# The twelve score matmuls of a pair of heads as one entry of the scheduler

## The chip, the cores and the metric

The kernel runs on one core of a Trainium2 chip. The metric is the device time of one execution in microseconds; lower is better. The engines of the core that matter here are TensorE (PE in the profile; its weight loads are PEld), VectorE (DVE), ScalarE (ACT), GpSimd (POOL) and SyncE (SP), which issues most of the DMAs. Each works through its own list of instructions in order, and semaphores make an instruction wait for results of other engines.

## What is computed

Two layers of a transformer encoder on 256 tokens of width 1024. Each layer is a mixer with three groups of attention heads of width 64, followed by a gated feed-forward part with a small convolution.

```
for l in range(DEPTH):                      # 2 layers
    # mixer: 4 neighbourhood heads (a), 6 dilated-window heads (d), 6 grouped-query heads (c)
    h = rms_norm(x, n1);  proj = h @ w_in_l
    qa, ka, va, qd, kd, vd, qc, kc, vc = jnp.split(proj, cuts, axis=-1)
    # per head: q and k are normalised (d and c also rotated), then
    #   s = q k^T * scale (+ bias or mask);  p = softmax(s);  o = p v
    mix = jnp.concatenate([rms_norm(out_a, ...), rms_norm(out_d, ...), rms_norm(out_c, ...)], axis=-1)
    x = x + mix @ w_out_l
    # feed-forward
    h = rms_norm(x, n2);  g, u = jnp.split(h @ w_gu, 2, axis=-1)
    g = depthwise_conv_centred(g, cw, cb)
    x = x + (gelu(g) * u) @ w_dn
```

Everything is float32. The kernel reaches that accuracy with matmuls on the type float32r: each operand is split into a high part and a remainder (hi and lo), and a product is the sum of hi x hi, hi x lo and lo x hi.

## The kernel before

**A planner orders all the work.** The kernel's code doesn't call the engines. `Plan.add` (L232) records each operation as an entry: its engine, its assumed duration (`cost`, L348), the earlier entries that it depends on, and its rank, which is its place in the program, moved back where the code says `later(n)`. `Plan.order` (L277) then simulates the engines. Again and again it looks at all entries whose predecessors are placed, and takes the one that can start earliest; among those that can start at the same time, the one of lowest rank. `emit` (L340) issues the operations in that order. So the order on each engine is fixed when the program is built, from assumed durations.

**Slots.** Tiles come from pools with a fixed number of slots. The slots of a pool are given out in a fixed turn, that of the tiles' first use in the program: an entry that would be the first user of a tile is not placed before all earlier tiles of that pool have their slot and one is free (L299 to L307). PSUM has two pools of four slots: `psa` for the accumulators of projections, and `psw` (tag `w`) for everything short-lived: the scores of a head (`s_`), the transposed probabilities (`tp_`), the output of a pair of heads (`o_`), transposes of q and k, and the gate and up products of the feed-forward part.

**A layer's mixer.** The projections are computed in the order dq, dk, dv, cq, ckv, aqk, av. A generator (`filler`, class `Weave`) yields them, and after them the output projections of the first two head groups (d and c), so that these matmuls stand between the steps of the attention. Attention goes through 16 heads, in the order d (6), c (6), a (4), by the loop at L1091. At step i (even) `scores(i)` writes the scores of heads i and i+1, `heads[i-1].turn()` transposes the probabilities of the head before, and `weigh(i-2)` multiplies those of the head before that with the values; each pair of heads shares an output tile, which `mixed` takes out. After the last head come `group_rstd(2)`, the output projections of the third group, and the feed-forward part.

**The scores of a pair** (L1023 to L1038). Two heads lie beside each other on the 128 partitions of q and k: the first on partitions 0 to 63 (`LOW`), the second on 64 to 127 (`HIGH`). Each head has 2 blocks of 128 queries, and each block three products, so 6 matmuls with 64 rows of contraction and 256 columns; the program lists the twelve of a pair with the two heads alternating. To the planner they are twelve separate entries with an assumed 60 ns each (the two lines in `cost` that test for rows up to `HD`). The first matmul of each head is the first user of that head's `psw` tile. `softens` then does the softmax: on DVE bias, sum and maximum (or only the maximum, for group c), on ACT the exponentials and the division by the sum.

Of the kernel before, what the change touches and what calls it, by code (L numbers as in the profile page):

```python
# [18 lines left out]
P = 128  # L19
S = 256  # L20
NT = S // P
D = 1024
KD = D // P
HD = 64
# [52 lines left out]
class View:  # L77


    def __init__(self, tile_, dtype, rows, idx, steps):  # L80
        self.tile, self.dtype, self.rows, self.idx, self.steps = tile_, dtype, rows, idx, steps
        self.shape, self.covers = (rows[1] - rows[0],) + idx.shape, None
# [111 lines left out]


class Op:
    __slots__ = ("engine", "method", "args", "kw", "ns", "size", "tiles", "first", "before", "after", "left", "at", "rank")


class PlanEngine:  # L200
# [14 lines left out]

class Plan:
    def __init__(self, tc):
        self.tc, self.ops, self.shift = tc, [], 0
        for name, short in (("tensor", "PE"), ("scalar", "ACT"), ("vector", "DVE"), ("gpsimd", "POOL"), ("sync", "SP")):
            setattr(self, name, PlanEngine(self, short, getattr(tc.nc, name)))  # L220

# [4 lines left out]
    def later(self, n):  # L226
# [2 lines left out]
        yield  # L229
        self.shift -= n  # L230

    def add(self, engine, method, args, kw):  # L232
        o = Op()
        o.engine, o.method, o.args, o.kw = engine, method, args, kw
        i = len(self.ops)
        o.rank = i + self.shift
        views = [v for v in (*args, *kw.values()) if isinstance(v, View)]
        outs = [v for v in args[:1] if isinstance(v, View)]
        if method == "tensor_tensor_reduce":
            outs.append(args[-1])  # L240
        if "accum_out" in kw:
            outs.append(kw["accum_out"])
        ins = [v for v in views if not any(v is w for w in outs)]
        if method == "matmul" and not kw["start"]:
            ins.append(args[0])
        o.ns, o.size = cost(engine.name, method, args, kw, ins)
        o.before, o.after, o.first, o.tiles = set(), [], [], []
        for v in ins + outs:
            t = v.tile
            if t not in o.tiles:  # L250
                o.tiles.append(t)
                t.users += 1
                if t.users == 1:
                    o.first.append(t)
        meets = lambda a, b: a[0] < b[1] and b[0] < a[1] and any(s < f and r < e for s, e in a[2] for r, f in b[2])
        holds = lambda a, b: a[0] <= b[0] and b[1] <= a[1] and len(a[2]) == 1 and a[2][0][0] <= b[2][0][0] and b[2][-1][1] <= a[2][0][1]
        for v in ins:
            f = v.footprint()
            met = {j for j, g in v.tile.writes if meets(f, g)}
            assert met, "read before written"  # L260
            o.before |= met
        for v in outs:
            f, t = v.footprint(), v.tile
            o.before |= {j for j, g in t.writes + t.reads if meets(f, g)}
            t.writes = [(j, g) for j, g in t.writes if not holds(f, g)]
            t.reads = [(j, g) for j, g in t.reads if not holds(f, g)]
        for v in ins:
            v.tile.reads.append((i, v.footprint()))
        for v in outs:
            v.tile.writes.append((i, v.footprint()))  # L270
        o.before.discard(i)
        o.left = len(o.before)
        for j in o.before:
            self.ops[j].after.append(i)
        self.ops.append(o)

    def order(self):  # L277
        ops = self.ops
        turns = {}
        for o in ops:  # L280
            for t in o.first:
                t.turn = turns.get(t.pool, 0)
                turns[t.pool] = t.turn + 1
                t.left = t.users
        free = dict.fromkeys(("PE", "ACT", "DVE", "POOL", "SP"), 550.0)
        ring = wires = 0.0
        ready = {e: [] for e in free}
        for i, o in enumerate(ops):
            o.at = 0.0
            if not o.left:  # L290
                ready[o.engine.name].append(i)
        done = []
        while len(done) < len(ops):
            best = None
            for e, r in ready.items():
                for i in r:
                    o = ops[i]
                    at = max(o.at, free[e])
                    for t in o.tiles:  # L299
                        s = t.pool  # L300
                        if t.slot is not None:
                            at = max(at, t.since)
                            continue
                        if t.turn != s.given or not s.free:
                            at = None
                            break
                        at = max(at, min(s.free)[0])  # L307
                    if at is not None and (best is None or (at, o.rank) < best[:2]):
                        best = (at, o.rank, i)
            at, _, i = best  # L310
            o = ops[i]
            e = o.engine.name
            ready[e].remove(i)
            done.append(i)
            for t in o.tiles:
                if t.slot is None:
                    s = t.pool
                    s.given += 1
                    place = min(s.free)
                    s.free.remove(place)  # L320
                    t.since, t.slot = place
            free[e] = end = at + o.ns
            if o.method == "dma_start":
                ring = max(at + 60, ring) + 460
                wires = max(ring + 550, wires) + o.size / 360
                end = wires + 900
            for t in o.tiles:
                t.left -= 1
                t.until = max(t.until, end)
                if not t.left:  # L330
                    t.pool.free.append((t.until + 170, t.slot))
            for j in o.after:
                a = ops[j]
                a.at = max(a.at, end + (170 if o.method == "dma_start" else HANDOVER.get((e, a.engine.name), 0)))
                a.left -= 1
                if not a.left:
                    ready[a.engine.name].append(j)
        return done

    def emit(self):  # L340
        real = lambda v: v.bind() if isinstance(v, View) else v
        with self.tc.manual_schedule():
            for i in self.order():
                o = self.ops[i]
                getattr(o.engine.real, o.method)(*map(real, o.args), **{k: real(v) for k, v in o.kw.items()})  # L345


def cost(engine, method, args, kw, ins):  # L348
# [6 lines left out]
    n = out.width()  # L355
    psum = any(v.tile.pool.psum for v in ins)
    if engine == "PE":
        if method == "transpose":
            return 110, 0
        n = args[2].width()  # L360
        if args[1].dtype == F32:
            return 108, 0
        if args[1].rows[1] - args[1].rows[0] <= HD:
            return 60, 0
        return (0.4444 * n + 4.6 if args[1].dtype == F32R else 210), 0
    if engine == "ACT":
        extra = 93 * sum(isinstance(kw.get(k), View) for k in ("scale", "bias")) + 90 * ("accum_out" in kw)
# [1 line left out]
    if engine == "DVE":  # L369
        if method in ("reduce_sum", "reduce_max"):  # L370
            n = args[1].width()
# [14 lines left out]
def encoder_kernel(  # L386
# [21 lines left out]
    nc = Plan(tc)  # L408
# [39 lines left out]
    with nc.later(1000):  # L448
        for _ in range(WARM):
            nc.tensor.matmul(  # L450
                wps.rearrange("p (a b) -> p a b", b=P), warm, warm.unsqueeze(1).to_broadcast([P, WARM_W // P, P]),
                start=True, stop=True,
# [15 lines left out]
    LOW, HIGH = slice(0, HD), slice(HD, P)  # L468
# [203 lines left out]
    for l in range(DEPTH):  # L672
# [350 lines left out]
        def scores(i):  # L1023

            two = heads[i : i + 2]
            group = two[0].group
            qs, ks = turned[group + "q"], turned[group + "k"]
            sps = [psw.tile([P, NT, S], F32, tag="w", name=f"s_{h.name}") for h in two]
            for t in range(NT):
                c = slice(t * P, (t + 1) * P)  # L1030
                for n, (x, y) in enumerate(((0, 0), (0, 1), (1, 0))):
                    for h, rows_, sp in zip(two, (LOW, HIGH), sps):
                        nc.tensor.matmul(
                            sp[:, t], qs[x][rows_, h.h // 2, c], ks[y][rows_, h.kv if group == "c" else h.h // 2],
                            start=n == 0, stop=n == 2,
                        )
            for h, sp in zip(two, sps):
                h.softens(sp)  # L1038

# [82 lines left out]
        _, r2 = mean_squares(f"n2{l}")  # L1122
# [188 lines left out]
```

## Time and profile before

| | |
|---|---|
| median of 3 runs | 633.17 us (632.21 to 633.89) |
| the profiled execution | 633.06 us, span 631.3 us, mean clock 0.997 |
| PE busy | 620.5 us (98% of the span), 3496 matmuls |
| DVE busy | 484.9 us (77%), 984 instructions |
| ACT busy | 429.6 us (68%), 1064 instructions |
| POOL busy | 72.2 us (11%) |
| score matmuls, both layers | 192 (120 of groups d and a, 72 of group c), 25.9 us busy |

In rows of the timeline the first number is the start in us from the beginning of the span, the second the length, then the engine, the line, the operation, the tile written, the tiles read, the shape, and how many instructions the row merges. All operations are issued at L345, so the line tells nothing here, and the tile names do: `psw_w` is a slot of the short-lived PSUM pool, `act_ko,act_qo` are keys and queries of groups d and a, `act_kc,act_qc` those of group c; a score matmul is recognised by its shape 64*128. `psa_a<-wp_hi,act_hT` is a projection, `psa_a<-wp_hi,act_mixT_hi` an output projection, `psw_w<-const_ident,act_s2k` a transpose of probabilities, and `psw_w<-act_ch,const_v` a weigh matmul. Matmuls overlap in the pipeline, so the distance from start to start says what one costs, not its own length.

### The profile page before, as it was taken

Reading aid. Unit: us, or ns where it says so; the run is one execution under the profiler, and the core shown is the slowest. Engines: PE = TensorE matmul, PEld = TensorE weight load, DVE = VectorE, ACT = ScalarE, POOL = GpSimd, SP = SyncE. Lnnn points to the kernel's source line nnn. Section 1 sums busy time; section 2 is a strip of 40 time slices with the busy share of each in tenths; the row PEclk is TensorE's granted clock in tenths of the full one; section 3 lists DMA queues with packets and bytes.
Section 4 is the critical chain, followed back from the end, with each engine's and each line's share of the span. In section 5 each row is a group of like instructions: output and inputs, shape, how many; then the busy total and the mean of one; then the engine's idle time right before and its main releaser. Section 6 shows DMA issues by size and latency. Waiting matters only on the chain.

```text
span 631.3 us, 9829 instructions
## 1 busy us (share of the span) xinstructions
PE 620.5 (98%) x3496; PEld 534.7 (85%) x3496; DVE 484.9 (77%) x984; ACT 429.6 (68%) x1064; POOL 72.2 (11%) x123
## 2 busy tenths in 40 slices
PE   8989999999999999999999999999999999999997
PEld 6988888878888888888899988888888888888886
DVE  4677987988777777777877798867887777777775
ACT  7578988767655566565678899985866555665552
POOL 3823231120000000000014212111100000000000
PEclk9989999999999999999999999999999999999999
DMA  9879220956656555665444731208565555565511
GB/s 293 271 199 201 72 73 14 227 199 202 200 200 200 180 176 182 197 200 184 129 125 165 250 102 50 67 5 267 191 209 201 182 174 182 195 198 177 174 53 66
DMA packets 84837, 104.66 MB, mean 166 GB/s; under 512 B 13012, under 2 KB 72500, under 8 KB 84788
## 3 DMA queue, kind: packets, MB, share of 16 engines
q1 hardware_dynamic: 84244, 103.51, 52.0%
q8 instruction: 27, 0.44, 0.3%
q10 hardware_dynamic: 544, 0.52, 0.3%
q14 instruction: 22, 0.18, 0.1%
HBM read 102.98 MB, written 1.49 MB: 165 GB/s over the span
## 4 chain that ended last, share of the span: by engine, by line
PE 84%; DVE 7%; ACT 3%; POOL 3%; issue 1%; DMA 1%; SPq 0%; DVEq 0%; ACTq 0%
PE psw_w L345 46%; PE psa_a L345 38%; DVE wp_lo L345 3%; ACT act_s2k L345 1%; DVE const_x L345 1%; DVE act_s2k L345 1%; POOL small_rstd L345 1%; DMA const_x<-in_x_dram 1%; DVE act_hT L345 1%; ACT wp_hi L345 1%; ACT L345 1%; POOL small_ms L345 1%; DVE act_nab L345 0%; SPq L345 0%; DVE act_qo L345 0%
## 5 line engine op out<-in xcount | busy, mean ns | idle before, releaser
L345 DVE TENSOR_TENSOR wp_lo<-wp_raw,wp_hi 128x512 fp32r<-128x512 f32 (+2 forms) x348 | 245.0, 733 | 62.3 <-ACT wp_hi L345 60.2
L345 PE MATMUL psw_w<-act_hT,wp_hi 128*128 128x512 f32 x704 | 249.2, 398 | 0.6 <-DVE act_hT L345 0.6
L345 ACT CAST wp_hi<-wp_raw 128x512 fp32r<-128x512 f32 (+2 forms) x348 | 212.9, 661 | 30.6 <-PE psw_w L345 15.9
L345 PE MATMUL psw_w<-act_hT,wp_lo 128*128 128x256 f32 x704 | 196.7, 281 | 0.1
L345 PEld LDWEIGHTS psw_w<-act_hT,wp_hi 128*128 128x128 f32 x704 | 131.8, 188 | 32.7 <-DVE act_hT L345 1.0
L345 PEld LDWEIGHTS psw_w<-act_hT,wp_lo 128*128 128x128 f32 x704 | 132.9, 189 | 1.9 <-DVE wp_lo L345 0.6
L345 PE MATMUL psa_a<-wp_hi,act_hT 128*128 128x384 f32 (+2 forms) x448 | 115.8, 338 | 1.4 <-ACT wp_hi L345 1.4
L345 ACT COPY act_s2k<-psw_w 128x256 f32<-128x256 f32 x88 | 32.4, 373 | 78.2 <-PE psw_w L345 78.2
L345 PEld LDWEIGHTS psa_a<-wp_hi,act_hT 128*128 128x128 f32 x448 | 79.1, 191 | 5.3 <-ACT wp_hi L345 1.8
L345 PE MATMUL psa_a<-wp_lo,act_hT 128*128 128x384 f32 (+2 forms) x224 | 75.7, 338 | 1.1 <-DVE wp_lo L345 1.0
L345 PE MATMUL psa_a<-wp_hi,act_cl 128*128 128x512 f32 x176 | 68.7, 392 | 0.6 <-DVE act_cl L345 0.6
L345 PE MATMUL psa_a<-wp_hi,act_ch 128*128 128x512 f32 x176 | 69.1, 393 | 0.0
L345 PE MATMUL psa_a<-wp_lo,act_ch 128*128 128x512 f32 x176 | 68.6, 390 | 0.0
L345 DVE TENSOR_TENSOR act_s2k<-psw_w,act_s2k 128x256 f32<-128x256 f32 x88 | 36.6, 422 | 31.0 <-ACT act_s2k L345 30.2
L345 PEld LDWEIGHTS psa_a<-wp_lo,act_hT 128*128 128x128 f32 x224 | 42.8, 191 | 3.4 <-DVE wp_lo L345 2.1
L345 PEld LDWEIGHTS psa_a<-wp_hi,act_cl 128*128 128x128 f32 x176 | 33.0, 188 | 8.8 <-DVE act_cl L345 1.4
L345 PEld LDWEIGHTS psa_a<-wp_hi,act_ch 128*128 128x128 f32 x176 | 33.0, 188 | 7.1
L345 PEld LDWEIGHTS psa_a<-wp_lo,act_ch 128*128 128x128 f32 x176 | 33.1, 188 | 6.4
L345 DVE SCALAR_TENSOR_TENSOR act_s2k<-act_s2k,act_cw,act_s2k 128x255 f32<-128x255 f32 x88 | 36.8, 480 | 1.4 <-ACT act_s2k L345 1.3
L345 ACT ACTIVATE act_s2k<-act_s2k,act_cw 128x256 f32<-128x256 f32 x44 | 24.1, 596 | 12.3 <-DVE act_s2k L345 12.3
L345 POOL TENSOR_TENSOR small_rstd<-small_ms,const_mh 128x6 f32<-128x6 f32 (+2 forms) x26 | 31.8, 1224 | 2.2
L345 ACT ACTIVATE act_s2k<-act_s2k,small_rs 128x256 f32<-128x256 f32 x64 | 29.0, 507 | 2.7 <-DVE small_rs L345 2.5
(109 smaller groups left out, 765.1 us busy)
## 6 DMA issues: line engine op xcount, KB each, us to landing
wp_raw<-in_w_gate_up_dram SPq DMA_DIRECT2D x44, 1024.0 KB, 5.1
wp_raw<-in_w_down_dram SPq DMA_DIRECT2D x22, 1024.0 KB, 5.0
wp_raw<-in_w_in_dram SPq DMA_DIRECT2D x14, 768.0 KB, 5.7
wp_raw<-in_w_in_dram SPq DMA_DIRECT2D x8, 1024.0 KB, 7.8
wp_raw<-in_w_out_dram SPq DMA_DIRECT2D x8, 768.0 KB, 5.5
wp_raw<-in_w_out_dram SPq DMA_DIRECT2D x4, 512.0 KB, 3.9
act_nab<-dram_scr SPq DMA_DIRECT2D x4, 448.0 KB
out_dram<-const_x SPq DMA_DIRECT2D x4, 256.0 KB, 2.0
```

The source lines that it names most:

```text
L345: getattr(o.engine.real, o.method)(*map(real, o.args), **{k: real(v) for k, v in o.kw.items()})
```

## The change

An entry of the planner can now hold several calls. The context manager `together(ns)` collects the operations recorded inside it and enters them as one entry with a given duration; `emit` issues its calls one behind the other. The rest of `add` becomes `enter`. In `order`, an entry may be the first user of several tiles: it is placed only when it is the turn of all of them and as many slots are free, at the time at which the last of these is free. `scores` wraps the twelve matmuls of a pair in `together(910)`, and the 60 ns of `cost` go away, since nothing uses them any more.

```diff
+    @contextmanager
+    def together(self, ns):
+        self.burst = calls = []
+        yield
+        self.burst = None
+        engine, method, args, kw = calls[0]
+        outs, ins = [], []
+        for _, _, a, _ in calls:
+            if not any(a[0] is v for v in outs):
+                outs.append(a[0])
+            ins += a[1:]
+        self.enter(engine, method, args, kw, ins, outs, calls, ns)
+
     def add(self, engine, method, args, kw):
-        o = Op()
-        o.engine, o.method, o.args, o.kw = engine, method, args, kw
-        i = len(self.ops)
-        o.rank = i + self.shift
+        if self.burst is not None:
+            self.burst.append((engine, method, args, kw))
+            return
...
+    def enter(self, engine, method, args, kw, ins, outs, calls, ns):
+        o = Op()
+        o.engine, o.method, o.calls = engine, method, calls
+        i = len(self.ops)
+        o.rank = i + self.shift
+        o.ns, o.size = (ns, 0) if ns else cost(engine.name, method, args, kw, ins)
...
                     at = max(o.at, free[e])
+                    news = {}
                     for t in o.tiles:
                         s = t.pool
                         if t.slot is not None:
                             at = max(at, t.since)
                             continue
-                        if t.turn != s.given or not s.free:
+                        n = news.get(s, 0)
+                        news[s] = n + 1
+                        if t.turn != s.given + n or len(s.free) <= n:
                             at = None
                             break
-                        at = max(at, min(s.free)[0])
+                        at = max(at, sorted(s.free)[n][0])
...
-                getattr(o.engine.real, o.method)(*map(real, o.args), **{k: real(v) for k, v in o.kw.items()})
+                for engine, method, args, kw in self.ops[i].calls:
+                    getattr(engine.real, method)(*map(real, args), **{k: real(v) for k, v in kw.items()})
...
-        if args[1].rows[1] - args[1].rows[0] <= HD:
-            return 60, 0
...
-            for t in range(NT):
-                c = slice(t * P, (t + 1) * P)
-                for n, (x, y) in enumerate(((0, 0), (0, 1), (1, 0))):
-                    for h, rows_, sp in zip(two, (LOW, HIGH), sps):
-                        nc.tensor.matmul(
-                            sp[:, t], qs[x][rows_, h.h // 2, c], ks[y][rows_, h.kv if group == "c" else h.h // 2],
-                            start=n == 0, stop=n == 2,
-                        )
+            with nc.together(910):
+                for t in range(NT):
+                    c = slice(t * P, (t + 1) * P)
+                    for n, (x, y) in enumerate(((0, 0), (0, 1), (1, 0))):
+                        for h, rows_, sp in zip(two, (LOW, HIGH), sps):
+                            nc.tensor.matmul(
+                                sp[:, t], qs[x][rows_, h.h // 2, c], ks[y][rows_, h.kv if group == "c" else h.h // 2],
+                                start=n == 0, stop=n == 2,
+                            )
```

More of the change, by code (lines that the diff above doesn't have):

```diff
@@ L196 @@
 class Op:
-    __slots__ = ("engine", "method", "args", "kw", "ns", "size", "tiles", "first", "before", "after", "left", "at", "rank")
+    __slots__ = ("engine", "method", "calls", "ns", "size", "tiles", "first", "before", "after", "left", "at", "rank")
 class PlanEngine:
@@ L217, in __init__ @@
     def __init__(self, tc):
-        self.tc, self.ops, self.shift = tc, [], 0
+        self.tc, self.ops, self.shift, self.burst = tc, [], 0, None
         for name, short in (("tensor", "PE"), ("scalar", "ACT"), ("vector", "DVE"), ("gpsimd", "POOL"), ("sync", "SP")):
@@ L245, in add @@
             ins.append(args[0])
-        o.ns, o.size = cost(engine.name, method, args, kw, ins)
+        self.enter(engine, method, args, kw, ins, outs, [(engine, method, args, kw)], 0)
+    def enter(self, engine, method, args, kw, ins, outs, calls, ns):
[4 more added lines that the diff above has]
+        o.ns, o.size = (ns, 0) if ns else cost(engine.name, method, args, kw, ins)
         o.before, o.after, o.first, o.tiles = set(), [], [], []
@@ L343, in emit @@
             for i in self.order():
-                o = self.ops[i]
-                getattr(o.engine.real, o.method)(*map(real, o.args), **{k: real(v) for k, v in o.kw.items()})
+                for engine, method, args, kw in self.ops[i].calls:
+                    getattr(engine.real, method)(*map(real, args), **{k: real(v) for k, v in kw.items()})
 def cost(engine, method, args, kw, ins):
```

## The prediction

> **What bounds the kernel now.** I read the page's totals first, then the busy time of every engine over the two attention stages, then TensorE's (PE's) instructions in order of time, looking for the score matmuls.
>
> ```profile
> span 631.3 us, 9829 instructions
> PE 620.5 (98%) x3496; PEld 534.7 (85%) x3496; DVE 484.9 (77%) x984; ACT 429.6 (68%) x1064; POOL 72.2 (11%) x123
> ```
>
> ```profile
> 49.70:120.30 70.60, 70.60 (x477) 60.83 (x477) 59.70 (x164) 60.94 (x179) 18.09 (x30) 1.00 0.44 101
> 357.80:426.80 69.00, 68.73 (x474) 59.14 (x474) 57.29 (x162) 62.06 (x180) 13.33 (x19) 1.00 0.19 61
> ```
>
> The second pair of rows runs from the first score matmul of a layer to the last weigh matmul: length, then busy time of PE, weight loads, DVE, ACT, POOL, then clock and DMA. PE has no gap in layer 0 and 0.27 us in layer 1, at full clock (1.00). DVE is busy 85% and 83%, ACT 86% and 90%. So PE sets the pace, but ACT stands close behind.
>
> Now the score matmuls. They are the only ones on 64 rows; a pair of heads uses rows 0-63 and 64-127. Rows of the timeline give start, length, shape, count:
>
> ```profile
> 49.77 0.98 PE L345 MATMUL psw_w<-act_ko,act_qo 64*128 64x256 f32 x12
> 50.67 0.39 PE L345 MATMUL psa_a<-wp_hi,act_hT 128*128 128x256 f32 x1
> ...
> 59.33 0.97 PE L345 MATMUL psw_w<-act_ko,act_qo 64*128 64x256 f32 x6
> 60.24 0.33 PE L345 MATMUL psw_w<-const_ident,act_z 128*128 128x128 f32 x1
> 60.49 0.97 PE L345 MATMUL psw_w<-act_ko,act_qo 64*128 64x256 f32 x6
> ...
> 80.95 0.38 PE L345 MATMUL psw_w<-act_kc,act_qc 64*128 64x256 f32 x1
> ```
>
> Twelve matmuls that alternate between the two row halves last as long (0.98) as six of one head alone (0.97). One alone lasts 0.38, so a run costs about 0.26 fixed plus 0.12 for each step, and in an alternating run a step carries two matmuls. A pair broken into two runs of six therefore pays for twelve steps where six would do.
>
> **The change, part by part.** It makes the twelve one entry, which nothing can split, placed when both PSUM slots are free. No instruction is added or removed and no DMA is issued anew; the order of everything after the first changed pair is chosen anew.
>
> *Score matmuls on PE.* The same view, restricted to the tiles of the keys (first the d and a heads, then the c heads; length and PE busy time are the first two values after the stretch):
>
> ```profile
> 45.00:110.00 65.00, 7.09 (x60) 5.44 (x60) 0.75 (x2) 0.65 (x2) 1.00 0.41 98
> 345.00:420.00 75.00, 8.31 (x60) 6.27 (x60) 1.85 (x4) 1.63 (x4) 1.00 0.30 100
> ...
> 45.00:110.00 65.00, 6.49 (x36) 4.67 (x36) 0.73 (x2) 0.61 (x2) 1.00 0.41 98
> 345.00:420.00 75.00, 4.02 (x36) 3.01 (x36) 0.85 (x2) 0.73 (x2) 1.00 0.30 100
> ```
>
> Layer 0 spends 7.09 + 6.49 = 13.58 us on scores, layer 1 8.31 + 4.02 = 12.33. Eight whole runs at 0.98 are 7.84 a layer: 5.74 and 4.49 less. Read in order, the runs count 12 | 6, 6 | 12 | 7, 5 | 1, 2, 3, 1, 5 | 6, 6 | 12 | 4, 2, 6 in layer 0 (17 runs for 8 pairs) and 12 | 12 | 3, 3, 6 | 1, 11 | 1, 11 | 12 | 6, 6 | 5, 1, 6 in layer 1 (15).
>
> Each run also slows its neighbours:
>
> ```profile
> 84.61 0.28 PE L345 MATMUL psw_w<-act_cl,const_v 128*128 128x256 f32 x1
> 84.73 0.28 PE L345 MATMUL psw_w<-act_ch,const_v 128*128 128x256 f32 x1
> 84.93 0.85 PE L345 MATMUL psw_w<-act_kc,act_qc 64*128 64x256 f32 x5
> 85.72 0.39 PE L345 MATMUL psa_a<-wp_lo,act_hT 128*128 128x256 f32 x1
> 85.94 0.40 PE L345 MATMUL psa_a<-wp_hi,act_hT 128*128 128x256 f32 x2
> ```
>
> A 128x256 matmul normally gives way after 0.12 (84.61 to 84.73). Ahead of the run it takes 0.20, behind it 0.22, which is 0.08 + 0.10 more; the run's last 0.06 overlaps its successor (84.93 + 0.85 - 85.72). Net 0.12 a run. Nine runs fewer in layer 0 are 1.1, seven in layer 1 are 0.8. PE work falls by 5.74 + 1.1 = 6.8 and 4.49 + 0.8 = 5.3, together 12.1 us. This part I hold for nearly certain; it would be the gain if PE stayed without gaps.
>
> *Where PE would run dry.* The planner has filler matmuls (projections, output projections of the first two head groups). If the attention chain ends no earlier, the saving can only be spent on filler that is still left when the last weigh matmul is done:
>
> ```profile
> 120.22 0.28 PE L345 MATMUL psw_w<-act_ch,const_v 128*128 128x256 f32 x1
> 120.33 0.40 PE L345 MATMUL psa_a<-wp_hi,act_mixT_lo 128*128 128x512 f32 x1
> ...
> 125.80 0.39 PE L345 MATMUL psa_a<-wp_hi,act_mixT_lo 128*128 128x512 f32 x1
> ```
>
> ```profile
> 121.36 0.48 DVE L345 SCALAR_TENSOR_TENSOR act_mixT_lo<-psw_w,const_gains,act_mixT_hi 128x256 fp32r<-128x256 f32 x1
> ```
>
> ```profile
> 120.30:133.70 13.40, 11.97 (x49) 8.86 (x49) 3.54 (x5) 0.00 (x0) 1.00 0.84 288
> 426.75:440.00 13.25, 12.23 (x50) 9.04 (x50) 4.18 (x6) 0.00 (x0) 1.00 0.96 316
> ```
>
> The last fence counts the output-projection matmuls (first value in brackets) after the last weigh: 49 and 50. The third head group owns 24 of them (2 blocks x 2 token tiles x 2 halves x 3 products); 25 and 26 are filler. At 24 steps in 5.47 us (120.33 to 125.80), or 0.228 each, that is 5.7 and 5.9 us of work in hand. Without it PE would stand from 120.33 until the third group's operand is written, 121.36 + 0.48 = 121.84: 1.5 us. With a chain that ends when it ends now, the cover is 5.7 - 1.5 = 4.2 of 6.8 us and, with the same 1.5, 5.9 - 1.5 = 4.4 of 5.3 us: 8.6 us together.
>
> *The chain itself can move either way.* It may come earlier, since DVE now stands waiting for scores:
>
> ```profile
> DVE small_nm L345 <- PE psw_w L345: 3.2, 5, 1.5
> DVE act_s2k L345 <- PE psw_w L345: 2.8, 4, 1.9
> ...
> DVE act_s2k L345 <- PE psw_w L345: 4.0, 5, 1.3
> DVE small_nm L345 <- PE psw_w L345: 1.1, 3, 0.6
> ```
>
> (two rows of layer 0, two of layer 1: total, times, longest.) Those 6.0 and 5.1 us are enough to let the whole 12.1 through. It may come later, since the first head of a pair now waits for the second head's slot. Queued behind that wait are, in the fixed turn of the PSUM slots, the transposes of the head before and the next output tile; but they wait today too, until the second head has its slot. Only the first head's softmax is new among the late ones. While PE holds an entry no other work can cut in, at most 0.91 us (49.77 to 50.67). I take the two shifts as cancelling; the bounds are +3.5 us of gain (12.1 - 8.6) and the delays of the second rival.
>
> *Crowding.* ACT's 62.06 us in layer 1 would have to fit into 69.0 - 4.4 = 64.6 us (96%); layer 0's 60.94 into 66.4 (92%). What PE loses beside a full ACT one stretch shows:
>
> ```profile
> 358.00:368.00 10.00, 9.73 (x78) 8.80 (x78) 8.36 (x29) 9.97 (x34) 2.64 (x3) 1.00 0.21 65
> ```
>
> 0.27 us of PE lost in 10 us with ACT at 9.97. Over the seven such stretches of a layer it is at most 1.9. I take half, 0.9, for layer 1, and nothing for layer 0, whose ACT would be less full; bounds 0 and 3.8 for both.
>
> *Sum.* 8.6 - 0.9 = 7.7 us. The profiled execution took 633.06 us (631.3 of span and 1.8 around it), 0.11 under the median of the runs shown, 633.17. 633.06 - 7.7 = 625.4 us.
>
> **The rivals.** *First, the freed PE time is partly given back.* The last pair of a layer decides when the chain ends, and its first head starts later:
>
> ```profile
> 105.93 0.74 PE L345 MATMUL psw_w<-act_ko,act_qo 64*128 64x256 f32 x4
> 108.75 0.97 PE L345 MATMUL psw_w<-act_ko,act_qo 64*128 64x256 f32 x6
> ```
>
> ```profile
> 412.57 0.85 PE L345 MATMUL psw_w<-act_ko,act_qo 64*128 64x256 f32 x5
> 415.37 0.97 PE L345 MATMUL psw_w<-act_ko,act_qo 64*128 64x256 f32 x6
> ```
>
> The start of its second head lies 2.8 us after that of its first in both layers. If both chains end that much later, the cover shrinks to 1.4 + 1.6 = 3.0 us: 630.1 us. For it: DVE and ACT then get two softmaxes at once. Against it: the second head, which ends the chain, gets its slot no later than now. The Trainium skill speaks for this rival (TensorEngine Tiling (Array Packing), section Performance Considerations, PSUM Bottleneck): tiling speeds up TensorE but not the emptying of PSUM, which may become the bound; by that rule the gain goes only as far as ACT and DVE have room, and no run here shows it yet.
>
> *Second, slower: the delays add up.* PSUM slots are given in a fixed turn, so a late first head can delay its transposes and, through them, the next pair. In layer 0 the second head starts 1.2 us after the first in the second pair (59.33 to 60.49), 2.9 in the fifth and 2.8 in the eighth; in layer 1 it is 3.9 in the third, 2.8 in the eighth:
>
> ```profile
> 83.85 0.38 PE L345 MATMUL psw_w<-act_kc,act_qc 64*128 64x256 f32 x1
> ...
> 372.34 0.61 PE L345 MATMUL psw_w<-act_ko,act_qo 64*128 64x256 f32 x3
> 376.20 0.97 PE L345 MATMUL psw_w<-act_ko,act_qo 64*128 64x256 f32 x6
> ...
> 406.37 0.97 PE L345 MATMUL psw_w<-act_ko,act_qo 64*128 64x256 f32 x6
> 409.11 0.97 PE L345 MATMUL psw_w<-act_ko,act_qo 64*128 64x256 f32 x6
> ```
>
> With 2.7 us for layer 1's seventh pair that is 6.9 + 9.4 = 16.3 us. It turns the result once more than the 7.7 us of cover, 47% of it, reaches the ends of the chains; if 80% does, 13.0 - 7.7 = 5.3 us are lost: 638.4 us. Against it: pairs that stood whole today (49.77) had both slots free anyway, and DVE's waits for scores are spread out, none over 1.9 us.
>
> *Third, no change.* The runs become whole, but the new order delays other work (transposes and weigh matmuls behind an entry: 16 entries at up to 0.91 us, 14.6 us at the most) by as much as it saves: about 633 us. Against it: PE is never idle at these places, so what waits is replaced by filler.
>
> **How the numbers follow.** The forecast 625.4 us has 0.66; its own range goes from the full 12.1 us (621.0) to half the gain (629.2). The first rival has 0.15, the second 0.11, the third 0.08. A measurement of this kernel can't tell less than 0.3% (1.9 us) from no change. Faster by more: 0.66 + 0.15 = 0.81; within: 0.08; slower: 0.11. The range reaches from 620.5 (the full saving and layer 1's idle 0.27 with it) to 632.5, past the first rival and into the third; the second stays outside.
>
> **What would show it.** Timeline: sixteen rows of twelve 64x256 matmuls of 0.98 us, none shorter in count; score busy time 15.7 us instead of 25.9. PE busy over the whole page near 609, DVE and ACT unchanged in count. After the last weigh matmul, fewer than 25 filler matmuls remain; if none remain and PE waits there for the mixed output, the first rival holds. The forecast is wrong if PE shows gaps within the attention stage ended by ACT or DVE, or if the last weigh matmul of a layer lies further behind its first score matmul than the present 70.6 and 69.0 us.

## The result and the profile after

The changed kernel takes 622.2 us (median of 4 runs, 621.25 to 623.27) beside 633.04 us for the kernel before: a ratio of 0.983, interval 0.981 to 0.985, so 10.8 us less. 7.7 us were forecast. The profiled execution took 621.25 us, its span 619.5.

The page's totals after the change:

```profile
span 619.5 us, 9832 instructions
PE 607.6 (98%) x3496; PEld 525.3 (85%) x3496; DVE 482.5 (78%) x984; ACT 428.3 (69%) x1064; POOL 73.6 (12%) x123
```

The same number of instructions on each of these engines, and PE busy 12.9 us less, in a span that is 11.8 us shorter. Where it went shows when each layer's mixer is cut at the same two instructions in both kernels, the first score matmul and the first matmul of the feed-forward part. First the kernel before, then the changed one (stretch, length, then busy time and number of instructions of PE, weight loads, DVE, ACT, POOL):

```profile
49.77:133.66 83.89, 83.37 (x539) 71.28 (x539) 70.81 (x182) 67.42 (x195) 20.80 (x33) 1.00 0.50 131
357.88:439.93 82.05, 81.65 (x536) 69.72 (x536) 67.16 (x180) 68.60 (x196) 15.75 (x22) 1.00 0.31 102
```

```profile
47.63:125.90 78.27, 77.33 (x539) 66.30 (x538) 70.28 (x183) 67.81 (x196) 21.08 (x33) 1.00 0.60 144
350.86:428.14 77.29, 76.73 (x536) 66.47 (x536) 66.23 (x180) 67.70 (x196) 16.11 (x22) 1.00 0.34 108
```

PE executes the same 539 and 536 matmuls, 6.04 and 4.92 us faster. The stretches get shorter by 5.62 and 4.76 us, 10.4 together; PE's idle time in them rises only from 0.92 to 1.50 us. The score matmuls of the changed kernel, in the views in which the prediction read them (the d and a heads, then the c heads):

```profile
45.00:110.00 65.00, 4.89 (x60) 3.87 (x60) 0.84 (x2) 0.86 (x2) 1.00 0.51 120
340.00:410.00 70.00, 4.90 (x60) 3.87 (x60) 1.77 (x4) 1.70 (x4) 1.00 0.33 107
...
45.00:110.00 65.00, 2.93 (x36) 2.31 (x36) 0.84 (x2) 0.72 (x2) 1.00 0.51 120
340.00:410.00 70.00, 2.94 (x36) 2.33 (x36) 0.84 (x2) 0.75 (x2) 1.00 0.33 107
```

15.66 us in place of 25.9. Each pair is one row of twelve, for instance the first, the third last and the last pair of layer 0:

```profile
47.64 0.98 PE L368 MATMUL psw_w<-act_ko,act_qo 64*128 64x256 f32 x12
...
94.29 0.98 PE L368 MATMUL psw_w<-act_kc,act_qc 64*128 64x256 f32 x12
...
106.28 0.98 PE L368 MATMUL psw_w<-act_ko,act_qo 64*128 64x256 f32 x12
```

What else differs between the two profiles is a small loss and a difference that isn't the change's. The loss: from the first matmul of layer 0's feed-forward part to the first scores of layer 1 it takes 0.74 us longer (224.96 us, before 224.22). 0.54 us of this come before the second half of the normalised input is there: PE now waits for it behind five weight splits on DVE. Two views of the changed kernel, DVE and PE (in brackets the idle time ahead of the row and who ended it), then the same matmul in the kernel before:

```profile
127.61 3.09 DVE L368 TENSOR_TENSOR wp_lo<-wp_raw,wp_hi 128x512 fp32r<-128x512 f32 x5
130.61 1.65 DVE L368 SCALAR_TENSOR_TENSOR act_hT<-psw_w,const_gains,act_hT 128x256 fp32r<-128x256 f32 x4
```

```profile
131.15 0.50 PE L368 MATMUL psw_w<-act_hT,wp_hi 128*128 128x512 f32 x1 [1.29 <-DVE act_hT L368]
```

```profile
138.37 0.50 PE L345 MATMUL psw_w<-act_hT,wp_hi 128*128 128x512 f32 x1 [0.28 <-DVE act_hT L345]
```

The other difference: the first score matmul starts 2.13 us earlier (49.77, now 47.64). In one repeat of the changed kernel it starts at 48.30, and in two kernels with the same order of work up to that point at 49.80 and 51.03, so this start scatters by itself. The granted clock is part of it. Before and after, the stretch ahead of the first scores (the clock is the value behind POOL's bracket):

```profile
36.00:47.60 11.60, 11.60 (x62) 11.57 (x61) 9.81 (x21) 8.02 (x19) 1.44 (x3) 0.85 0.84 214
```

```profile
36.00:47.60 11.60, 11.60 (x70) 11.35 (x68) 9.54 (x21) 9.12 (x29) 1.87 (x5) 1.00 0.90 216
```

The kernel before was profiled with the clock at 0.85 there, the changed one at 1.00; if PE's work goes with the clock, that is (1.00 - 0.85) x 11.6 = 1.7 us, an estimate. The stages account for 10.38 - 0.74 = 9.64 us, which lies inside the interval (9.5 to 12.2 us). Below, a kernel is judged by its median and by the sum of its two stretches, which differs by 0.05 us between the two profiles of the changed kernel: 165.94 us before, 155.56 after, 155.61 in the repeat. Part of the scatter of the medians goes with the clock. With a mean granted clock below 0.998 the kernel before, as it ran beside the experiments, has a median of 633.6 us (32 executions), with a higher one 632.6 (9); the changed kernel and its repeat together have 623.6 (3) and 621.9 (5). At like clock that is 10.0 and 10.7 us less, from few executions.

### The profile page after: what moved, and what is told of

Its sections match the earlier page's. It is cut to its first block, busy times and chain, and to the rows that moved or that the text cites. A ratio compares the mean times of both kernels' runs of the same rounds, so it can differ in the third digit from the quotient of the medians.

```text
span 619.5 us, 9832 instructions
## 1 busy us (share of the span) xinstructions
PE 607.6 (98%) x3496; PEld 525.3 (85%) x3496; DVE 482.5 (78%) x984; ACT 428.3 (69%) x1064; POOL 73.6 (12%) x123
## 4 chain that ended last, share of the span: by engine, by line
PE 84%; DVE 7%; ACT 3%; POOL 3%; issue 2%; DMA 1%; SPq 0%; DVEq 0%; ACTq 0%
PE psw_w L368 45%; PE psa_a L368 39%; DVE wp_lo L368 3%; ACT act_s2k L368 2%; POOL small_rstd L368 1%; DVE const_x L368 1%; DVE act_s2k L368 1%; DMA act_s2k<-in_norm_g_dram 1%; DVE act_hT L368 1%; ACT L368 1%; POOL small_ms L368 0%; DVE act_z L368 0%; DVE act_qo L368 0%; POOL act_sck L368 0%; DVE act_cl L368 0%
## 5 line engine op out<-in xcount | busy, mean ns | idle before, releaser
L368 ACT ACTIVATE act_s2k<-act_s2k,act_cw 128x256 f32<-128x256 f32 x44 | 24.1, 596 | 12.9 <-DVE act_s2k L368 12.9
L368 ACT ACTIVATE act_s2k<-act_s2k 128x512 f32<-128x512 f32 x22 | 13.9, 632 | 22.3 <-DVE act_s2k L368 22.3
```

Of the source, the lines that this page charges most:

```text
L368: getattr(engine.real, method)(*map(real, args), **{k: real(v) for k, v in kw.items()})
```

## The experiments

Beside the repeat, only the first two variants below keep the changed kernel's order of everything else. Each of the others has an order of its own, and an order by itself moves the time by several us, as the experiments with the declared duration show. So a difference of 2 us between two orders doesn't prove its cause. What holds across all of them is PE's work: in the two stretches PE is busy from 153.7 to 166.3 us, and idle for 0.8 to 2.7 us in all kernels but one (4.3 us, declared with 720 ns).

**The same order of work without the alternation.** If the gain is PE time, it must go when the two heads no longer alternate, though everything else stays in its place.

```diff
             with nc.together(910):
-                for t in range(NT):
-                    for n, (x, y) in enumerate(((0, 0), (0, 1), (1, 0))):
-                        for h, rows_, sp in zip(two, (LOW, HIGH), sps):
+                for h, rows_, sp in zip(two, (LOW, HIGH), sps):
+                    for t in range(NT):
+                        for n, (x, y) in enumerate(((0, 0), (0, 1), (1, 0))):
```

> One entry per pair and both slots at once, as in the changed kernel, but within the entry all six matmuls of the first head come before the six of the second, so the two row halves no longer alternate. The declared 910 ns stays, so the order on every engine is that of the changed kernel. Theory (the gain is PE time, because alternating matmuls share a step): a run has 12 steps, 0.26 + 12 x 0.12 = 1.70 us in place of 0.98, 16 x 0.72 = 11.5 us more PE work than the changed kernel: 622.2 + 11.5 = 633.7, about the time of the kernel before. Rival (the gain comes from the order that the planner now finds, not from the alternation): 622 to 625.

Measured: 628.7 us, ratio 0.993 (0.990 to 0.995), stretches 159.95. By the medians more than half of the gain is gone, by the stretches 4.4 of 10.4 us, by the order of twelve matmuls alone. But it is some 6 us and not 11.5. The run is shorter than I had worked out:

```profile
51.03 1.32 PE L368 MATMUL psw_w<-act_ko,act_qo 64*128 64x256 f32 x12
```

1.32 us, not 1.70. With that the sum comes out between the two measures: 16 x 0.34 = 5.4 us, against 4.4 us in the stretches and 5.9 to 6.5 in the medians (622.8 and 622.2 for the changed kernel). The forecast time failed for its price of a run; the theory that PE time sets the pace stands, and the rival (622 to 625) is out.

**Where the short run comes from.** In the serial run three of the twelve starts coincide with another. Either PE itself takes matmuls of the other half ahead, or three overlap wherever the halves change.

```diff
             with nc.together(910):
                 for t in range(NT):
-                    for n, (x, y) in enumerate(((0, 0), (0, 1), (1, 0))):
-                        for h, rows_, sp in zip(two, (LOW, HIGH), sps):
+                    for h, rows_, sp in zip(two, (LOW, HIGH), sps):
+                        for n, (x, y) in enumerate(((0, 0), (0, 1), (1, 0))):
```

> The changed kernel with its twelve in blocks of three: three of the first head, three of the second, and again; the order of everything else is that of the changed kernel. The serial order of six and six took 1.32 us a run and not the 1.70 that twelve steps would give: three of its twelve starts coincide with another. Theory A (TensorE itself takes matmuls of the other half ahead, up to three behind a change of halves from the first to the second): nearly all find a partner, a run of 0.98 to 1.1 us, 622 to 624.5. Theory B (three coincide per run, wherever the halves change): 1.3 us a run and 628 to 629, like the serial order. Theory C (only neighbours in the list can coincide): three changes of halves, three coincidences, the same 1.3 us and 628 to 629; the starts in the trace tell B and C apart.

Measured: 623.5 us, ratio 0.984 (0.983 to 0.986), stretches 155.75. Theory A:

```profile
49.80 0.98 PE L368 MATMUL psw_w<-act_ko,act_qo 64*128 64x256 f32 x12
```

The starts of the twelve, read from the trace (us, from the first):

```
alternating     0.000 0.004  0.225 0.227  0.341 0.345  0.466 0.470  0.580 0.583  0.699 0.702
threes          0.000 0.010  0.223 0.233  0.340 0.350  0.465 0.475  0.579 0.589  0.698 0.708
six and six     0.000  0.223  0.340 0.348  0.465  0.571 0.579  0.690 0.698  0.808  0.928  1.048
```

Three and three pair off as completely as one and one. With six and six, the second half begins to pair at the third step. The record of a matmul doesn't name its half, so which two coincide is read from the lists. The lengths in the records agree with it: in each run just two are 0.38 us long, as the first of a half is, and these are the first two records of the alternating runs and the threes, but the first and the fourth (0.000 and 0.348) of six and six.

**The same serial entry, declared longer.** Does the planner's knowledge of the duration matter? Here the serial entry is declared longer (its real length turned out to be 1.32 us, so 1630 is too much).

```diff
-            with nc.together(910):
+            with nc.together(1630):
```

> The same as the serial entry, but declared with 1630 ns, about what it really takes, so the planner lays the rest around it accordingly. Theory: the PE work is that of the serial entry, so 632 to 634, at most 1.5 us better than with the wrong declaration. Rival (what matters is that the declared duration is right): clearly faster than the entry declared with 910 ns, 626 or less.

Measured: 631.1 us, ratio 0.996 (0.995 to 0.998), stretches 163.51: 2.4 us worse than the same run declared with 910. Its score matmuls take the same 21.2 us. But PE is busy for 160.81 us of the stretches against 159.12 with 910, and idle for 2.70 us against 0.83. So the rest of the order costs here: 1.7 us more busy time in other matmuls and 1.9 us more waits. The forecast range (632 to 634) was missed by 0.9 us; the rival (626 or less) is out.

**The kernel before with truer durations.** The 60 ns per matmul were too low for a run of one head (0.12 us a step); without the two lines a score matmul counts 118 ns.

```diff
-        if args[1].rows[1] - args[1].rows[0] <= HD:
-            return 60, 0
```

> The kernel before with one thing changed: the 60 ns that the planner assumes for a score matmul become 118, which is what one of a single head takes. Entries stay single. In this order the score matmuls stand in 30 runs (before 32) with 132 steps (before 146), 16 x 0.12 + ... of them: 30 x 0.38 + 132 x 0.12 = 27.2 us of PE against 29.7 before. Theory: 633.0 - 2.5 x 0.9 = 630.8 us. Rival (truer durations are the gain): 622 to 625. A rival that durations do nothing and the order only shifts: 633.

Measured: 632.7 us beside 633.6, ratio 0.999 (0.997 to 1.001), stretches 165.43. No difference that can be told, which is the last of the three expectations; the score matmuls take 24.5 us instead of 25.9. The theory's 630.8 was 2 us too low, and the rival that truer durations are the gain is out by 8 us.

**No joint wait: one entry per head.** This takes away what both of the prediction's rivals rest on, the first head's wait for the second head's slot.

```diff
-            with nc.together(910):
-                for t in range(NT):
-                    for n, (x, y) in enumerate(((0, 0), (0, 1), (1, 0))):
-                        for h, rows_, sp in zip(two, (LOW, HIGH), sps):
+            for h, rows_, sp in zip(two, (LOW, HIGH), sps):
+                with nc.together(910):
+                    for t in range(NT):
+                        for n, (x, y) in enumerate(((0, 0), (0, 1), (1, 0))):
```

> Each head is an entry of its own: its six matmuls stand together, and it takes only its own slot, so the first head never waits for the second head's slot; the halves don't alternate. In this order there are 23 runs and 192 steps: 23 x 0.38 + 192 x 0.12 = 31.8 us of PE, 14.2 more than the changed kernel, 2.7 more than the serial entry with both slots at once. If waiting for both slots costs nothing: 2.4 to 2.7 us above the serial entry declared truly, so 635 to 637. If the joint wait costs several us (the rivals of the prediction): at or below that entry's time, 633 or less.

Measured: 634.9 us, ratio 1.003 (1.002 to 1.004), stretches 167.74: slower than the kernel before, though no work can cut into a head's six. Its score matmuls take 26.4 us in 23 runs, those of the serial entry 21.2 us in 16; with 0.12 us a run the difference is 6.0 us of PE work. Beside the serial entry declared with 1630, 3.8 us are measured by the medians and 4.2 by the stretches, so by that comparison the joint wait costs some 2 us over 16 pairs. Beside the one declared with 910 it is 6.2 us, and the wait costs nothing. Two orders can differ by that much, so a cost of the joint wait isn't shown; a large one is out, and what it brings (the halves side by side) is worth more, even when the list is serial.

**Both slots at once, but not uncut.** Only the first matmul of each head share an entry.

```diff
-            with nc.together(910):
...
+            with nc.together(310):
+                for k in calls[:2]:
+                    one(*k)
+            for k in calls[2:]:
+                one(*k)
```

> Only the first two matmuls of a pair, one of each head, are one entry (310 ns), which takes both slots; the other ten stay single entries of 60 ns that other work may cut into. In this order there are 19 runs, all of them alternating (three pairs are cut 2 + 10), against 16 in the changed kernel: 3 x 0.38 = 1.1 us more PE work. Theory (taking both slots at once is what makes the halves alternate, and being uncut is worth little): 623.3 us, 622.0 to 624.5. Rival (the uncut run is the main part): 626 or more.

Measured: 621.9 us (0.1 below the forecast range), ratio 0.982 (0.981 to 0.983), stretches 154.89. As good as the changed kernel (repeat below) though three pairs are cut and the score matmuls take 16.4 us instead of 15.7. Being one uncut run adds nothing that can be measured: that both heads have their slot when the first matmul starts is enough for the gain. (`calls` is the list of the twelve in the old order, `one` issues one of them; the 60 ns stay.)

**The changed kernel again, as a measure.**

> The changed kernel once more, as the measure for the runs beside it on the same chip: 622.2 us within 1.5, ratio to the kernel before 0.983.

Measured: 622.8 us, ratio 0.984 (0.982 to 0.986).

**A fourth slot in layer 0.** The tile of the warming matmuls keeps one of the four slots until its last three are done, at 83 us.

```diff
-WARM, WARM_W = 28, 256
+WARM, WARM_W = 25, 256
```

> The changed kernel without the last three of 28 warming matmuls, which compute nothing that is used and keep one of the four short-lived PSUM slots of layer 0 until 83 us. Theory of the slots (waiting for two slots costs in the first pairs, where only three are left): layer 0's attention gets shorter, 620 to 621.5. Theory that PE work alone counts: 0.4 us of PE less, 621.8, no difference that can be told.

Measured: 621.3 us, ratio 0.982 (0.980 to 0.983). Layer 0's stretch falls from 78.29 to 77.53 us, layer 1's stays (77.32 and 77.33). Of the 0.8 us the three matmuls themselves are 0.5. Both theories named a time that it fits; against the repeat it isn't told apart, and a large cost of waiting for slots is not in it. The slot does move the attention: layer 0's last weigh matmul comes 64.78 us after the first scores, 3.4 us earlier than in the repeat (68.18). That this brings 0.8 us says that the end of the attention chain hardly bounds the changed kernel here.

**The declared duration.** Longer and shorter than the 910 ns.

```diff
-            with nc.together(910):
+            with nc.together(1030):
```

and, in another kernel,

```diff
-            with nc.together(910):
+            with nc.together(720):
```

> The changed kernel with a declared duration of 1030 ns (0.91 from start to start and 0.12 for the slowed neighbours) in place of 910. If the plan's agreement with the real durations matters: 1 to 2 us faster, 620.5 to 621.5. If not: 622.2 within 1.5.

> The changed kernel with a declared duration of 720 ns, twelve times the 60 of the kernel before, in place of 910. The longer declaration of 1030 took 624.6 us beside 622.8 for 910. If a longer declaration is what costs: 620 to 621.5. If each declaration only gives another order among many of about the same worth: 621 to 625, with no trend.

Measured: 1030 gives 624.6 us, ratio 0.986 (0.984 to 0.988); 720 gives 627.3 us, ratio 0.990 (0.988 to 0.992). Neither expectation holds. With 1030 the median is 1.8 us above the repeat, with intervals that overlap, and the stretches (156.67) are 1.1 us longer; 720 loses nearly half the gain (stretches 159.74), with sixteen whole runs and 15.8 us of score matmuls. Why the planner's order is worse there is open; three durations can't tell a rule from chance. The shorter declaration brings out something near what the prediction called its first rival. After the last weigh matmul of layer 0:

```profile
49.59:120.28 70.69, 70.37 (x502) 60.76 (x502) 62.27 (x169) 62.75 (x183) 18.67 (x30) 1.00 0.53 123
120.28:131.40 11.12, 8.30 (x40) 6.35 (x38) 10.52 (x18) 7.06 (x16) 2.49 (x3) 0.89 0.66 225
```

```profile
128.40 0.44 PE L368 MATMUL psw_w<-const_ident,const_x 128*128 128x128 f32 x2 [1.79 <-DVE const_x L368]
129.06 1.54 PE L368 MATMUL psw_w<-const_ident,const_x 128*128 128x128 f32 x6 [0.22 <-DVE const_x L368]
131.41 0.79 PE L368 MATMUL psw_w<-act_hT,wp_hi 128*128 128x512 f32 x1 [0.81 <-DVE act_hT L368]
```

The chain ends 70.7 us after the first scores, as before the change. The output projections left at that point number 24, as many as the third group owns: the filler is used up. PE runs these 24 without a gap; then it stands, 2.8 of the 11.1 us, for the residual (`const_x`) and the normalised input (`act_hT`), while DVE is busy for 10.5 us, and the clock is 0.89 over these 11.1 us. DVE's largest groups there:

```profile
L368 DVE TENSOR_TENSOR wp_lo<-wp_raw,wp_hi 128x512 fp32r<-128x512 f32 x6 | 4.5, 768 | 0.0
L368 DVE SCALAR_TENSOR_TENSOR const_x<-psa_a,small_rstd,const_x 128x512 f32<-128x512 f32 x6 | 4.1, 742 | 0.6 <-POOL small_rstd L368 0.6
L368 DVE SCALAR_TENSOR_TENSOR act_nab<-act_nab,const_na 128x1728 f32<-128x1728 f32 x1 | 1.9, 1946 | 0.0
```

Layer 1's stretch is 77.93 us, nearly the changed kernel's.

**Two level variants together.** Both slots at once without the uncut run, and 25 warming matmuls (the two diffs above).

> The two variants that came out level with the changed kernel or a little ahead (621.9 and 621.3), together: only the first two matmuls of a pair are one entry, and the last three warming matmuls, whose result is not used, are left out. In this order there are 21 runs, all alternating, five of them cut 2 + 10. If both small gains are real and add: 620 to 621. If they are another order of the same worth, and each cut costs 0.38 us: 622 to 624.

Measured: 622.2 us, ratio 0.983 (0.981 to 0.985), stretches 156.11. The small gains don't add; the second expectation (622 to 624) holds. No variant is clearly ahead of the changed kernel.

## Why the prediction was right, and where its size was off

**PE work: right.** Sixteen rows of 0.98 us and 15.7 us of score matmuls were forecast; there are sixteen, and 15.66. The neighbours included, 12.1 us were forecast; PE is busy 6.04 + 4.92 = 11.0 us less in the two stretches. The score matmuls alone fell by 10.25 us, 10.23 were forecast. So the missing 1.1 us lie beside them, where 1.9 us were forecast and 0.7 came: in other matmuls (the changed order puts other shapes side by side) or in the 0.12 us a run; no run tells which.

**The cover: the step that failed.** Of the chain I wrote that I take its two shifts, earlier and later, as cancelling, and so let only 8.6 of 12.1 us through. They don't cancel. The last weigh matmul stood 70.45 and 68.77 us behind the first score matmul; now it is 68.17 and 65.36. The last weigh matmul of layer 1 before and after, then that of layer 0 after, and what follows the ten output projections behind it:

```profile
426.66 0.28 PE L345 MATMUL psw_w<-act_ch,const_v 128*128 128x256 f32 x1
```

```profile
416.22 0.28 PE L368 MATMUL psw_w<-act_ch,const_v 128*128 128x256 f32 x1
```

```profile
115.81 0.28 PE L368 MATMUL psw_w<-act_ch,const_v 128*128 128x256 f32 x1
...
118.22 0.50 PE L368 MATMUL psw_w<-const_ones,act_sqm 128*128 128x1 f32 x4
```

So 2.3 and 3.4 us of the saving come through the chain itself, and only the rest is paid from filler: behind the last weigh matmul 34 and 44 output projections are left, 24 of them counted as the third group's, so 10 and 20 filler matmuls (25 and 26 before). The traces point to the waits of DVE for scores, 6.0 and 5.1 us before, as the reason; no experiment singles it out. What is left of them, layer 0 and then layer 1:

```profile
DVE small_nm L368 <- PE psw_w L368: 0.7, 1, 0.7
DVE act_s2k L368 <- PE psw_w L368: 0.4, 1, 0.4
...
DVE act_s2k L368 <- PE psw_w L368: 0.4, 1, 0.4
```

Not all of that is won: DVE's waits for ACT up to the last weigh matmul rise from 3.5 to 6.7 us in layer 0 and from 4.7 to 7.7 in layer 1, most of it in these two rows:

```profile
DVE act_cl L368 <- ACT act_ch L368: 1.8, 3, 0.8
...
DVE act_cl L368 <- ACT act_ch L368: 2.4, 2, 1.8
```

The prediction had these waits as the bound that lets everything through, and should have taken its side: the second head, which ends a pair, gets its slot no later than before, and its scores are done in 0.98 us with the first head's instead of behind them. The first head's later start, which I set against it, has no large cost (one entry per head, without that wait, was slower).

**Crowding: near in size by luck, in another place.** 0.9 us were taken, for layer 1 and beside a full ACT. There PE's idle time rises by only 0.16 us, and its one longer wait for ACT from 0.3 to 0.4. In layer 0, where nothing was taken, it rises by 0.42, and 0.74 us are lost behind its attention, where PE waits for DVE: 1.3 us in all. One of layer 0's waits lies within the attention:

```profile
86.83 0.51 PE L368 MATMUL psa_a<-wp_hi,act_mixT_hi 128*128 128x512 f32 x1 [0.45 <-DVE act_z L368]
```

By its letter that is a sign that the prediction named for being wrong; at 0.45 us it didn't decide.

**The sum.** Of the 12.1 us forecast, 11.0 came as busy time, 10.4 in the stretches and 9.6 with the loss behind, against 7.7. So the errors partly cancelled: 1.1 us too much PE work and 0.4 too little crowding against 3.5 us held back by the cover that weren't lost. The medians say 10.8, or 10.0 to 10.7 at like clock; the rest between them and the stages is within the interval and, with one profile of the kernel before and a scattering start, stays open.

**The rivals.** The first (freed time given back) did not happen here, but in part in the kernel declared with 720 ns: there layer 0's chain ends no earlier and no filler is left. PE doesn't wait for the mixed output, as the rival had it, but behind the last output projection. So the 1.5 us a layer that the prediction took off its cover, PE standing until the third group's operand is written, aren't seen in the one stretch that could show them. The rule of the Trainium skill beside this rival (TensorEngine Tiling (Array Packing), section Performance Considerations, PSUM Bottleneck) is not shown by any run: in that stretch more than half of DVE's 10.5 busy us are weight splits and a bias, which empty no PSUM. In the changed kernel PE stays busy 98.8% and 99.3% of the stretches. The second (delays add up) is out: both chains end earlier. The third (no change) is out.

## What to carry to other kernels

Where an engine does two things at once only if they stand near each other in its list, a scheduler that places them one by one loses that whenever a resource for one of them comes later; make it take both resources before the first is placed. And when work is taken off the engine that sets the pace, look at the chain that feeds the end of the stage before deciding how much comes through: here the waits of DVE for scores were the hint that the chain would come earlier too. A planner's order is sensitive to the durations that it is told: 0.91 us, the length from start to start, was better than 0.72 by 5 us and than 1.03 by 2 us, though a truer duration of the single matmuls brought nothing. So compare several orders before a gain of 2 us is put down to a change.

## What the hardware showed unexpectedly

TensorE doesn't need the alternation in the list. With three matmuls of one row half and then three of the other, all start in pairs 4 to 14 ns apart, in a run of 0.98 us; with six and six, three pairs form and the run takes 1.32 us. The kernel before had one such run (layer 1, third pair of group c), which the prediction counted as whole:

```profile
401.02 1.32 PE L345 MATMUL psw_w<-act_kc,act_qc 64*128 64x256 f32 x12
```

On the lists and starts that are there, a matmul of one half starts before earlier ones of the other half have started, up to three places ahead in the list; so across the two halves TensorE does not keep to the order of its list. How far it can look was not tried beyond three and six.
